# Two hybrid trunk layers on one core: the output projection in one pass over its weights, adaLN moved into the mixers

## The chip, the cores and the metric

The kernel runs on one NeuronCore of a Trainium2 chip. The metric is device time in microseconds. In the text PE is TensorE, DVE is VectorE, ACT is ScalarE, POOL is GpSimd, and SP is the engine whose queue issues every DMA of this kernel.

## The reference, cut to what matters

Five tiles of 128 tokens (tile 0 the prompt, tiles 1 to 4 the samples), 1024 wide, go through two layers. `m` has six vectors of 1024 for each of the two conditions (prompt and sample).

```python
def trunk_layer(x, cond, lp, ctx):
    m = silu(cond) @ lp['w_ada'] + lp['b_ada']          # adaLN
    sh1, sc1, g1, sh2, sc2, g2 = jnp.split(m, 6, axis=-1)
    h = layer_norm(x) * (1.0 + sc1) + sh1
    o, new_ctx = mixing(h, lp, ctx)                     # S5 scan | neighbourhood attention | GQA, then @ w_out
    x = layer_norm(DEEPNORM_ALPHA * x + g1 * o, lp['ln1_g'], lp['ln1_b'])
    h = layer_norm(x) * (1.0 + sc2) + sh2
    a, gate = jnp.split(h @ lp['w_ffn_in'], 2, axis=-1)
    f = (silu(a) * gate) @ lp['w_ffn_out']
    x = layer_norm(DEEPNORM_ALPHA * x + g2 * f, lp['ln2_g'], lp['ln2_b'])
    return x, new_ctx
```

## The kernel before

Every product of fp32 operands is made of three matmuls of a high and a low part (`mm3`, L309), so each weight block that arrives is split (`split`, L280): a copy on ACT makes the high part, a subtraction on POOL or DVE the low part. `wload` (L293) loads 512 KB into one of three `wr` buffers and splits it into two blocks in the `wh` and `wl` rings of seven each.

One layer runs like this (`layer`, L1349). First come 18 GQA units (`pipelined`), and after each of them `between` (L1405) gives out some steps of the scan, of the remaining input projections and, at units 6 to 11 of layer 0, the six adaLN units in `todo`. Then comes neighbourhood attention (NA) in ten units with the rest of the scan between them. Then `wout` (L1463), then `ffn` (L1716). A unit of adaLN (`ada`, L358) is one vector and one half: eight slices of w_ada of 256 KB, 32 small matmuls, a PSUM copy on ACT, a transpose, an addition on DVE. After the second half of vector 2 or 5 (the gates) a copy on DVE, another transpose, a second copy and a DMA store the gate rows.

`wout` works in two groups, tiles 2, 1, 0 and then 3, 4. For each group and each half of 512 columns it loads and splits all of w_out's blocks for that half, four loads of 512 KB, and multiplies. The results are gated and added to the residual on DVE (L1497, L1498). Then follow for each tile of the group `post_ln` (L1277), a second normalisation, and `ffn_in_tile` (L1535), which transposes, modulates, and builds the operands of the FFN. Between the second group's matmuls and its LayerNorms stand three adaLN units (L1500; one word: `ADAW`), vector 5 of this layer and the start of the next layer's. In layer 1 only two are left.

`ffn` runs 22 blocks of `ffn_in` (the first two by `ffn_in_plain`, whose first halves need only tiles 2, 1 and half of 0) in six parts; after each part its share of w_ffn_out is applied to all tiles: a multiplication by the gate row and an addition per tile and half, both on DVE (L1755 to L1762). From the third block on one step of `ffn_side` is given out per block: one adaLN unit (up to vector 4 of the next layer) and one step of the scan's tables.

The order of instructions on each engine is that of the program, changed by the framework's planner, which runs a timeline of its own with priorities (attention units have a higher one). Each engine and SP's queue then keep their order.

Of the kernel before, what the change touches and what calls it, by code (L numbers as in the profile page):

```python
# [16 lines left out]
D = 1024  # L17
# [140 lines left out]
class Build:  # L158
# [7 lines left out]
    ADAN = (0,) * 6 + (1,) * 6 + (0,) * 6  # L166
# [126 lines left out]
    def wload(self, src, lo_eng=None):  # L293
# [8 lines left out]
        return [self.wsplit(raw[:, c:c + 512], lo_eng) for c in range(0, n, 512)]  # L302

    def wsplit(self, src, lo_eng=None):
        hi, lo = [self.wp.tile([128, 512], F32R, name=self.nm(t), tag=t, bufs=self.NW) for t in ("wh", "wl")]
        self.split(src, hi, lo, lo_eng)
        return hi, lo
# [50 lines left out]
    def ada(self, l, M, vec, half, wide=None, side=False):  # L358
# [35 lines left out]
        if vec in (2, 5) and half == 1:  # L394
            gc = self.smallp.tile([128, 2, KD], F32, name=self.nm("gc"), tag="gc", bufs=1)
            nc.vector.tensor_copy(gc, modc[:, vec].rearrange("p k c -> p c k"))
            pt = bank[0:16, 256:384]
            nc.tensor.transpose(pt, gc.rearrange("p c k -> p (c k)"), self.ident)
            row = (self.ev(n=128) if side else self.zt(128))[0:16]
            nc.vector.tensor_copy(row, pt)  # L400
            nc.sync.dma_start(gates[vec // 3].rearrange("c (k p) -> (c k) p", p=128), row)
# [947 lines left out]
    def layer(self, l, A, xsrc, T, nxt, tab, todo):  # L1349
# [55 lines left out]
        def between(n):  # L1405
# [12 lines left out]

        self.pipelined(units, 1, between)
        for _ in fill:  # L1420
            pass
        Ns = [self.na_prep(l, 0, zqk[0], znv)]
# [23 lines left out]
        for _ in ssm:  # L1446
            pass
        return self.wout(l, M, mx, xsrc, nxt)
# [14 lines left out]
    def wout(self, l, M, mx, xsrc, nxt):  # L1463
# [6 lines left out]
        ada = self.ada_side(l, M, nxt)  # L1470
        self.function(AF.Silu, self.after)
# [6 lines left out]
        junk = None  # L1478
        for group in self.GROUPS:
            for i in group:  # L1480
                xs[i] = self.k4()
                nc.sync.dma_start(xs[i], xsrc[i])
                sums[i] = self.columns("wsum")
            for n in range(2):
                cs = slice(n * 512, (n + 1) * 512)
                s2 = self.psS()
                ps = [s2[:, 0], s2[:, 1]] + ([self.psM()] if len(group) == 3 else [])
                for j, pair in enumerate((2, 3, 0, 1)):
                    w = self.wload(I["w_out"][l, pair // 2, n, pair % 2], self.LO[j % 2] and G)
                    for p, i in zip(ps, group):  # L1490
                        a = slice(i * 128, (i + 1) * 128)
                        for kk in range(2):
                            k = 2 * pair + kk
                            self.mm3(p, mh[:, k, a], ml[:, k, a], *w[kk], j + kk == 0, j + kk == 4)
                for p, i in zip(ps, group):
                    cd = 0 if i == 0 else 1
                    V.tensor_tensor(out=p, in0=p, in1=row(("g", cd), M["gates"][0, cd])[:, cs], op=ALU.mult)  # L1497
                    self.residual(xs[i][:, cs], p, sums[i][n], ALPHA)  # L1498
            self.ada_wide = False
            for _ in range(self.ADAW[min(self.GROUPS.index(group), 1)]):  # L1500
                next(ada, None)
            self.ada_wide = True
            for i in group:
                get = self.xs if i < 3 else self.ys
                xn = get(n=512), get(n=512)
                junk = junk or (self.k4(),)
# [397 lines left out]
```

## Time and profile before

| | us |
|---|---|
| median of 3 runs | 1804.81 (1793.88 to 1805.54) |
| profiled execution | 1804.75 |
| its span, first to last instruction | 1802.7 |
| PE busy | 1655.2 (92%) |
| DVE busy | 1224.2 (68%) |
| ACT busy | 822.3 (46%) |
| POOL busy | 762.5 (42%) |
| mean granted clock | 0.95 |

The page shows the busy share of each engine in 40 slices of 45 us, and the granted PE clock as a share of full speed (0.5 is 1.2 GHz, 1.0 is 2.4 GHz). The windows give the same sums for any stretch, the waits who stood still for whom, and the orders of time single instructions.

### The profile page before, as it was taken

How to read it: one execution, taken by the hardware profiler on the slowest of the kernel's cores; microseconds unless marked ns; L12 is line 12 of the kernel's file. 1: busy time of each engine (PE TensorE's matmuls, PEld its weight loads, DVE VectorE, ACT ScalarE, POOL GpSimd, SP SyncE). 2: the span in 40 equal slices, each digit the busy share in tenths (PEclk: the TensorE clock that was granted, in tenths of full speed). 3: DMA queues.
4: the chain of work that ended last, by engine and by line, in shares of the span. 5: the costliest groups of instructions: out<-in, count | busy, mean ns of one | idle time of the engine just before them, and what ended most of it. 6: DMA issues, size and time to landing. Idle time of an engine off the chain costs nothing.

```text
span 1802.7 us, 31473 instructions
## 1 busy us (share of the span) xinstructions
PE 1655.2 (92%) x11624; PEld 1447.3 (80%) x11624; DVE 1224.2 (68%) x2460; ACT 822.3 (46%) x1796; POOL 762.5 (42%) x651
## 2 busy tenths in 40 slices
PE   5889899898899999999898989998979999999997
PEld 3778677676688888898797978976759898998995
DVE  5576536646778777678877555565476787876777
ACT  5435445556542334243246446665564342432433
POOL 3753303048434334346266232210684464363453
PEclk8889899889899999999999989998989999999999
DMA  8434767545453545332324243463542232222312
GB/s 311 121 110 116 231 202 203 149 158 178 149 161 115 176 126 184 109 115 72 122 77 165 91 115 86 121 183 113 178 161 83 91 98 64 89 74 68 105 60 82
DMA packets 183114, 234.90 MB, mean 130 GB/s; under 512 B 78960, under 2 KB 112048, under 8 KB 182960
## 3 DMA queue, kind: packets, MB, share of 16 engines
q1 hardware_dynamic: 182960, 232.88, 42.3%
q8 instruction: 92, 1.51, 0.3%
q14 instruction: 62, 0.51, 0.1%
HBM read 203.57 MB, written 29.39 MB: 129 GB/s over the span
## 4 chain that ended last, share of the span: by engine, by line
PE 66%; DVE 12%; DMA 10%; ACT 4%; issue 3%; POOL 2%; SPq 1%; POOLq 0%; DVEq 0%; ACTq 0%
PE psM L311 9%; PE psM L312 9%; PE psM L313 9%; PE psT L311 6%; PE psT L312 6%; PE psT L313 5%; DMA ev<-in_w_ada_dram 3%; PE psT L859 3%; PE psS L311 2%; PE psS L312 2%; PE psS L313 2%; PE psS L1157 2%; DMA wr<-in_w_ffn_in_dram 2%; PE psT L1184 2%; POOL wl L284 2%
## 5 line engine op out<-in xcount | busy, mean ns | idle before, releaser
L284 POOL TENSOR_TENSOR wl<-wr,wh 128x512 fp32r<-128x512 f32 x362 | 502.1, 1406 | 523.8 <-ACT wh L283 341.6
L283 ACT CAST wh<-wr 128x512 fp32r<-128x512 f32 x450 | 275.0, 620 | 388.4 <-PE psM L313 91.3
L311 PE MATMUL psM<-hh,wh 128*128 128x320 f32 x560 | 178.1, 318 | 2.5 <-DVE ev L400 1.2
L312 PE MATMUL psM<-hl,wh 128*128 128x320 f32 x560 | 176.2, 315 | 0.3 <-POOL hl L284 0.3
L313 PE MATMUL psM<-hh,wl 128*128 128x320 f32 x560 | 176.2, 315 | 0.0
L311 PEld LDWEIGHTS psM<-hh,wh 128*128 128x128 f32 x560 | 107.1, 191 | 5.5 <-DVE ev L400 1.8
L311 PE MATMUL psT<-hh,wh 128*128 128x320 f32 x352 | 110.0, 312 | 0.0
L312 PE MATMUL psT<-hl,wh 128*128 128x320 f32 x352 | 109.1, 310 | 0.0
L313 PE MATMUL psT<-hh,wl 128*128 128x320 f32 x352 | 109.0, 310 | 0.0
L313 PEld LDWEIGHTS psM<-hh,wl 128*128 128x128 f32 x560 | 107.0, 191 | 1.7 <-issue 1.6
L312 PEld LDWEIGHTS psM<-hl,wh 128*128 128x128 f32 x560 | 107.2, 191 | 1.1 <-POOL hl L284 0.6
L230 POOL TENSOR_TENSOR sm<-sm,mhalf 128x1 f32<-128x1 f32 (+2 forms) x46 | 55.9, 1217 | 96.3 <-DVE sm L260 51.7
L1638 DVE TENSOR_TENSOR ys<-ys,psM 128x320 f32<-128x320 f32 x140 | 65.0, 482 | 34.7 <-PE psM L313 32.9
L1638 DVE TENSOR_TENSOR ys<-ys,psT 128x320 f32<-128x320 f32 x140 | 65.1, 481 | 30.4 <-PE psT L313 29.0
L1160 DVE TENSOR_REDUCE psS<-psS 128x1 f32<-128x640 f32 x64 | 52.8, 828 | 45.3 <-PE psS L1157 43.7
L311 PE MATMUL psT<-b,wh 128*128 128x320 f32 x240 | 76.6, 319 | 7.3 <-DVE ys L1638 7.2
L311 PE MATMUL psM<-b,wh 128*128 128x320 f32 x240 | 76.4, 318 | 5.7 <-DVE ys L1638 5.6
L284 POOL TENSOR_TENSOR wl<-ws,wh 128x512 fp32r<-128x512 f32 x40 | 53.6, 1341 | 62.7 <-ACT wh L283 62.6
L311 PE MATMUL psM<-wh,hh 128*128 128x256 f32 (+1 forms) x232 | 73.8, 318 | 6.1 <-DVE sm L1329 2.9
L311 PE MATMUL psM<-wh,xs 128*128 128x512 f32 x190 | 75.1, 395 | 3.5 <-DVE k L1762 2.8
L311 PE MATMUL psT<-wh,xs 128*128 128x512 f32 x190 | 75.3, 396 | 2.9 <-DVE k L1762 2.9
L859 PE MATMUL psT<-ident,ys 128*128 128x128 f32 x440 | 75.4, 291 | 2.7 <-ACT ys L290 1.0
(439 smaller groups left out, 4904.8 us busy)
## 6 DMA issues: line engine op xcount, KB each, us to landing
wr<-in_w_ffn_in_dram SPq DMA_DIRECT2D x88, 512.0 KB, 3.8
ev<-in_w_ada_dram SPq DMA_DIRECT2D x112, 256.0 KB, 4.0
wr<-in_w_ffn_out_dram SPq DMA_DIRECT2D x40, 512.0 KB, 3.9
wr<-in_w_out_dram SPq DMA_DIRECT2D x32, 512.0 KB, 3.6
wr<-in_w_in_dram SPq DMA_DIRECT2D x28, 512.0 KB, 4.4
wa<-in_w_ada_dram SPq DMA_DIRECT2D x24, 512.0 KB, 4.6
k<-in_x_dram SPq DMA_DIRECT2D x10, 512.0 KB, 5.6
xs<-zqk SPq DMA_DIRECT2D x32, 160.0 KB, 5.1
```

The lines of the kernel that those rows point to most:

```text
L230: self.nc.gpsimd.tensor_tensor(out=o, in0=v, in1=self.mhalf.broadcast_to([128, v.shape[1]]), op=ALU.pow)
L283: nc.scalar.copy(hi, src)
L284: (lo_eng or nc.vector).tensor_tensor(out=lo, in0=src, in1=hi.bitcast(F32), op=ALU.subtract)
L311: nc.tensor.matmul(ps, lhsT=ah, rhs=bh, start=first, stop=False)
L312: nc.tensor.matmul(ps, lhsT=ah, rhs=bl, start=False, stop=False)
L313: nc.tensor.matmul(ps, lhsT=al, rhs=bh, start=False, stop=last)
L859: self.nc.tensor.transpose(pt[:, j * 128:(j + 1) * 128], s, self.ident)
L1157: nc.tensor.matmul(sp[:, b, 0:320], lhsT=qT[:, h * 128:(h + 1) * 128], rhs=kx[kv][:, b * 320:(b + 1) * 320], start=st, stop=en)
L1160: V.tensor_reduce(out=m, in_=sp[:, :, 0:320], axis=AX.XY, op=ALU.max, negate=True)
L1184: nc.tensor.matmul(pt[hh * 64:hh * 64 + 64, 256:384], lhsT=K["v"][:, j, kv * 64:kv * 64 + 64], rhs=PTs[j // 2][:, c0:c0 + 128], start=(j = ...
L1638: V.tensor_tensor(out=o, in0=x, in1=y, op=ALU.add)
```

## The change

- `wout` first multiplies the first half of the columns for all five tiles in five PSUM banks (one pass over half of w_out), then splits the second half's eight blocks and keeps them: seven in the rings, one in an `ev` buffer. The second half is multiplied for one tile at a time, in the order 2, 1, 0, then 3 and 4 between the LayerNorms of 2, 1 and 0.
- No adaLN stands in `wout`. Vectors 2, 3 and 4 are made in each layer's own mixers: a generator gives out parts of two slices after the GQA units from unit 5 on, each loaded one step ahead into a `wr` buffer, and parts of four slices in the ring buffers during NA. Each part ends with its own copy, transpose and addition. FFN's side now has vector 5 of its layer and vectors 0 and 1 of the next.
- The FFN's output sum is kept ungated: part 0 copies it on ACT, parts 1 to 3 add, part 4 adds, multiplies by the gate row and adds ALPHA times the saved tile, part 5 is as before. The tile is saved to DRAM (`xd`) after its LayerNorm and reloaded by halves in part 4.

```diff
-    ADAN = (0,) * 6 + (1,) * 6 + (0,) * 6
+    ADA0 = 5
...
+    def ada_parts(self, l, M, todo):
...
+        for vec, half in todo:
...
+            while k0 < KD:
+                n = 4 if self.ada_free else 2
...
+                    raw = self.wp.tile([128, n, 512], F32, name=self.nm("wa"), tag="wr", bufs=self.NRAW)
+                    nc.sync.dma_start(raw, wv[:, k0:k0 + n, c0:c0 + 512])
...
+                yield
+                bank = self.psM()
...
+                mrow = self.zt(128)
+                nc.scalar.copy(mrow, ps)
+                nc.tensor.transpose(pt, mrow, self.ident)
...
+            if vec == 2 and half == 1:
+                self.gate_rows(M, vec, bank, self.zt)
...
-            for _ in range(self.ADAN[n]):
-                if todo:
-                    self.ada(l, M, *todo.pop(0))
+            if n >= self.ADA0:
+                next(ada, None)
...
-        for _ in ssm:
+            if n:
+                next(ada, None)
+        for _ in itertools.chain(ada, ssm):
...
-        for group in self.GROUPS:
...
+        s2 = self.psS(), self.psS()
+        ps = [s[:, b] for s in s2 for b in range(2)] + [self.psM()]
+        pairs = 2, 3, 0, 1
+        for j, pair in enumerate(pairs):
+            w = pair, self.wload(I["w_out"][l, pair // 2, 0, pair % 2], G)
+            for p, i in zip(ps, self.WORD):
+                product(p, i, w, j == 0, j == 3)
+        ws = [(pair, self.wload(I["w_out"][l, pair // 2, 1, pair % 2], G, self.ev if j == 3 else None))
+              for j, pair in enumerate(pairs)]
+        for p, i in zip(ps, self.WORD):
+            gated(0, i, p)
...
+        def second(i):
+            p = self.psM()
+            for j, w in enumerate(ws):
+                product(p, i, w, j == 0, j == 3)
+            gated(1, i, p)
+
+        def through(i):
...
+            nc.sync.dma_start(xd[i], xs[i])
+            self.ffn_in_tile(xn, i, M["modc"], H)
...
+        for i in self.WORD[:3]:
+            second(i)
+        for m, i in enumerate(self.WORD):
+            through(i)
+            for k in self.WORD[m + 3:m + 4]:
+                second(k)
...
+    WORD = (2, 1, 0, 3, 4)
...
+                x = xs[i][:, cs]
                 if part == 0:
...
+                    S.copy(x, ps)
+                elif part < len(PARTS) - 2:
+                    V.tensor_tensor(out=x, in0=ps, in1=x, op=ALU.add)
                 else:
...
+                        t = self.zt()
+                        nc.sync.dma_start(t, xd[i][:, cs])
+                        V.tensor_tensor(out=ps, in0=ps, in1=x, op=ALU.add)
+                        V.tensor_tensor(out=ps, in0=ps, in1=g[:, cs], op=ALU.mult)
+                        V.scalar_tensor_tensor(out=x, in0=t, scalar=ALPHA, in1=ps, op0=ALU.mult, op1=ALU.add)
...
-            for vec in range(5):
+            for vec in range(2):
...
-            todo = [(2 + n // 2, n % 2) for n in range(6)]
             for l in range(L):
+                todo = [(2 + n // 2, n % 2) for n in range(6)]
```

## Rows read from the trace of the kernel before

**Rows 1.** Page: busy tenths of PE in 40 slices, and the granted clock

```profile
PE   5889899898899999999898989998979999999997
PEclk8889899889899999999999989998989999999999
```

**Rows 2.** Windows: stretch, length, busy us (instructions) of each engine, clock, DMA share, GB/s

```profile
413.40:487.00 73.60, 59.20 (x428) 45.61 (x427) 59.78 (x120) 47.38 (x89) 51.68 (x41) 0.86 0.57 183
438.50:476.50 38.00, 23.60 (x234) 16.05 (x235) 32.03 (x68) 24.52 (x48) 24.45 (x21) 0.77 0.62 196
1322.60:1358.50 35.90, 23.70 (x206) 17.14 (x205) 27.16 (x63) 23.77 (x47) 25.27 (x22) 0.76 0.52 166
310.00:360.00 50.00, 41.65 (x286) 31.21 (x286) 34.87 (x100) 27.87 (x80) 3.42 (x9) 0.83 0.62 163
1060.00:1200.00 140.00, 137.33 (x1225) 122.92 (x1224) 80.61 (x213) 88.86 (x227) 32.02 (x42) 0.98 0.40 110
1200.00:1260.00 60.00, 53.23 (x332) 40.13 (x330) 37.95 (x101) 32.63 (x94) 5.67 (x10) 0.80 0.53 151
```

**Rows 3.** Order of time on PE: start us, us, line, operation, tiles, shape

```profile
437.88 0.39 PE L312 MATMUL psS<-wl,hh 128*128 128x512 f32 x1
438.11 0.39 PE L313 MATMUL psS<-wh,hl 128*128 128x512 f32 x1
...
456.00 0.90 PE L311 MATMUL psS<-hh,wh 128*128 128x320 f32 x2
...
502.35 0.31 PE L312 MATMUL psM<-hl,wh 128*128 128x320 f32 x1
502.49 0.31 PE L313 MATMUL psM<-hh,wl 128*128 128x320 f32 x1
...
1322.27 0.39 PE L313 MATMUL psS<-wh,hl 128*128 128x512 f32 x1
```

**Rows 4.** Waits of PE, 440:480 and 1326:1362: us in total, times, longest

```profile
PE psM L381 <- DMA ev<-in_w_ada_dram: 12.1, 7, 3.4
...
PE psM L381 <- DMA ev<-in_w_ada_dram: 8.2, 4, 3.5
```

**Rows 5.** Order of time on DVE: the plain FFN blocks' last multiplications

```profile
503.92 0.49 DVE L1712 TENSOR_TENSOR ys<-psT,ys 128x320 f32<-128x320 f32 x1
...
1382.28 0.48 DVE L1712 TENSOR_TENSOR ys<-psT,ys 128x320 f32<-128x320 f32 x1
```

**Rows 6.** Groups by shape, DVE, 410:490: count, busy us, mean ns, idle before

```profile
L1298 DVE SCALAR_TENSOR_TENSOR k<-k,sm,k 128x1024 f32<-128x1024 f32 x5 | 10.1, 2027 | 2.3 <-POOL sm L230 2.2
L1288 DVE SCALAR_TENSOR_TENSOR k<-k,sm,k 128x1024 f32<-128x1024 f32 x5 | 8.1, 1610 | 0.0
```

**Rows 7.** Instructions of L1298: duration min/median/max ns, first and last start us

```profile
L1298 DVE SCALAR_TENSOR_TENSOR k<-k,sm,k x19: 1274/1286/2315, 419.4 to 1794.8; 128x1024 f32<-128x1024 f32 x19
```

**Rows 8.** Chain that ended last, 440:480: start us, us, what

```profile
451.65 0.23 PE psM L386
...
461.65 0.57 PE psM L381 x16
```

**Rows 9.** Waits of PE, 140:320: us in total, times, longest

```profile
PE psM L381 <- DMA wa<-in_w_ada_dram: 5.0, 4, 3.2
PE psM L386 <- ACT zt L385: 5.0, 2, 3.1
PE psM L398 <- DVE gc L396: 2.0, 1, 2.0
```

**Rows 10.** Waits of PE, 480:960: us in total, times, longest

```profile
PE psS L381 <- DMA ev<-in_w_ada_dram: 4.2, 8, 1.5
PE psM L311 <- DVE k L1762: 2.8, 2, 2.5
```

**Rows 11.** Groups by line: count, busy us, mean ns, idle before and releasers

```profile
L284 POOL TENSOR_TENSOR wl<-wr,wh 128x512 fp32r<-128x512 f32 x362 | 502.1, 1406 | 523.8 <-ACT wh L283 341.6
...
L1755 DVE TENSOR_TENSOR psM<-psM,k 128x512 f32<-128x512 f32 x50 | 34.8, 695 | 26.6 <-PE psM L313 26.4
```

More of the change, by code (lines that the diff above doesn't have):

```diff
@@ L290, in evac, with wload @@
             self.nc.scalar.copy(out, in_)
-    def wload(self, src, lo_eng=None):
+    def wload(self, src, lo_eng=None, last=None):
         nc = self.nc
@@ L301, in wload, with wsplit @@
         nc.sync.dma_start(rv, src)
-        return [self.wsplit(raw[:, c:c + 512], lo_eng) for c in range(0, n, 512)]
-    def wsplit(self, src, lo_eng=None):
-        hi, lo = [self.wp.tile([128, 512], F32R, name=self.nm(t), tag=t, bufs=self.NW) for t in ("wh", "wl")]
+        return [self.wsplit(raw[:, c:c + 512], lo_eng, last if c + 512 >= n else None) for c in range(0, n, 512)]
+    def wsplit(self, src, lo_eng=None, place=None):
+        if place:
+            hi, lo = place(F32R), place(F32R)
+        else:
+            hi, lo = [self.wp.tile([128, 512], F32R, name=self.nm(t), tag=t, bufs=self.NW) for t in ("wh", "wl")]
         self.split(src, hi, lo, lo_eng)
@@ L394, in ada @@
         if vec in (2, 5) and half == 1:
[L395 to L401, printed above, removed]
+            self.gate_rows(M, vec, bank, self.ev if side else self.zt)
@@ new lines, in gate_rows @@
+    def gate_rows(self, M, vec, bank, place):
+        nc = self.nc
+        gc = self.smallp.tile([128, 2, KD], F32, name=self.nm("gc"), tag="gc", bufs=1)
+        nc.vector.tensor_copy(gc, M["modc"][:, vec].rearrange("p k c -> p c k"))
+        pt = bank[0:16, 256:384]
+        nc.tensor.transpose(pt, gc.rearrange("p c k -> p (c k)"), self.ident)
+        row = place(n=128)[0:16]
+        nc.vector.tensor_copy(row, pt)
+        nc.sync.dma_start(M["gates"][vec // 3].rearrange("c (k p) -> (c k) p", p=128), row)
@@ L1470, in wout @@
         ada = self.ada_side(l, M, nxt)
+        xd = self.dp.tile([NT, 128, D], F32, name=self.nm("xd"))
         self.function(AF.Silu, self.after)
@@ L1476, in row @@
             return rows[key]
-        junk = None
-        for group in self.GROUPS:
[L1480 to L1506, printed above, removed]
-                s = self.post_ln(xs[i], row("lg", I["ln1_g"][l]), row("lb", I["ln1_b"][l]), sums[i], junk,
-                                 self.LNW[i])
-                self.normalise(xs[i], xn, self.stats_of(xs[i], s, junk, "lsn"), self.NORMV[2])
-                self.ffn_in_tile(xn, i, M["modc"], H)
@@ L1511, in wout, with product @@
-        return self.ffn(l, xs, M, H, nxt, ada)
-    LO = (True, True)
-    GROUPS = ((2, 1, 0), (3, 4))
-    ADAW = (0, 3)
+        for i in self.WORD:
+            xs[i] = self.k4()
+            nc.sync.dma_start(xs[i], xsrc[i])
+            sums[i] = self.columns("wsum")
+        def product(p, i, w, first, last):
+            pair, blocks = w
+            a = slice(i * 128, (i + 1) * 128)
+            for kk in range(2):
+                k = 2 * pair + kk
+                self.mm3(p, mh[:, k, a], ml[:, k, a], *blocks[kk], first and kk == 0, last and kk == 1)
@@ new lines, in gated @@
+        def gated(n, i, p):
+            cs, cd = slice(n * 512, (n + 1) * 512), 0 if i == 0 else 1
+            V.tensor_tensor(out=p, in0=p, in1=row(("g", cd), M["gates"][0, cd])[:, cs], op=ALU.mult)
+            self.residual(xs[i][:, cs], p, sums[i][n], ALPHA)
+        s2 = self.psS(), self.psS()
[5 more added lines that the diff above has]
+                product(p, i, w, j == 0, j == 3)
@@ L1728, in ffn @@
         f0 = 0
-        for key, cd in (("gp", 0), ("gs", 1)):
-            row(key, M["gates"][1, cd])
         for part, nf in enumerate(PARTS):
```

54 lines of the change are left out of this document (45 added, 9 removed).

## The prediction

> **What bounds the kernel now.** I read the page first. TensorE (PE) stands at 8 or 9 tenths and more in nearly all of its slices [rows 1], so the time is its matmul stream plus the places where that stream stops or runs at the lower clock. In the page's slices PE and PEclk dip together around the end of each layer's output projection, in layer 0's attention, and at the ends of the run [rows 1]. So next the windows by stage [rows 2]: 1060 to 1200 us (layer 1's GQA units) is 98% PE, with nothing to hide new PE work behind; 310 to 360 and 1200 to 1260 us (the neighbourhood attention, NA, of the two layers) leave 8.4 and 6.8 us idle; the two stretches from the projection's last matmul to a full FFN stream, 438.5 to 476.5 and 1322.6 to 1358.5 us, leave 14.4 and 12.2 us idle and run at a mean clock of 0.77 and 0.76. The third view, PE's order of time, shows what stands in the first of these [rows 3]: the last projection matmul starts at 438.11, the first FFN product only at 456.00. The fourth, PE's waits there, names one releaser: the adaLN matmuls that the kernel queues at that place wait 12.1 and 8.2 us for their 256 KB weight loads [rows 4]. That view alone would promise 20 us. The fifth view, VectorE (DVE), says why it is not all to be had: from 413.4 to 487.0 us it is busy 59.8 of 73.6 us, 81% [rows 2], with the post-LayerNorm and FFN operands of five tiles. The FFN's first two blocks (the plain ones) are through at 503.92 and 1382.28 [rows 5]; these are the marks by which I measure a shorter tail.
>
> **The change part by part.** The sum is made against the profiled execution, 1804.75 us (span 1802.7 and 2.05 around it); the median of the runs shown is 1804.81, the same.
>
> *A. Projection and tail.* Matmuls stay 240 a layer. What goes: 8 of 16 loads of 512 KB and 16 of 32 weight splits a layer, each 1406 ns on GpSimd (POOL) [rows 11], 22.5 us a layer, and the adaLN units there (three in layer 0, two in layer 1). POOL and the loads are not what PE waits for while it projects, so for themselves they are worth nothing; they count through DVE, below. The new order ends its first-half pass 120 matmuls before the end. At 0.23 us each [rows 3] that is 438.3 - 27.6 = 410.7, and 1322.5 - 27.6 = 1294.9 in layer 1. Tile 2's second half is then complete 5.5 us later, the others every 5.5 us. Now DVE has all the LayerNorm work ahead of it: 59.8 us, plus 4.3 for six first-half operations of three tiles that were done earlier (3 x two of 0.7), less 6.3 that belongs after tile 4's first operand: 57.8. Of this, 5.5 us is stretching: the 1024-wide LayerNorm operations mean 2027 ns, or 1610 [rows 6], where the shortest takes 1274 [rows 7], five of each kind. So the work is 57.8 at the old share of 81%, 71.4 us, at worst, and 52.3 us at 100% at best. I take 52.3 at 92% (halfway between the tail's own 84% [rows 2] and full), 57 us, because POOL, whose splits ran beside the slow ones, loses 22.5 us just there. Then 2 us for the operand's split, and the plain blocks' second halves, 96 matmuls at 0.147 [rows 3], 14.1 us, and 1 us to the mark: 410.7 + 57 + 2 + 14.1 + 1 = 484.8 against 503.9, -19; in layer 1, 1369 against 1382.3, -13. A = **-32**, ends -42 (52.3) and -4 (71.4). The first halves fill part of the wait from about 447 on. The first FFN weights can be split only as the held second half comes free (8 splits, 11 us of POOL from about 434): done by 446, just hidden; uncovered, up to 6 us.
>
> The slow operations are those with two inputs in SBUF while POOL works. The Trainium skill ("SBUF — State Buffer", Who interferes with whom) says that a VectorE instruction with two SBUF inputs and a GpSimd instruction that reads SBUF exclude each other for a whole instruction. The trace agrees as far as 1274 against up to 2315 ns goes [rows 7]. By that rule the FFN's weight splits, now run beside the LayerNorms of tiles 0, 3 and 4, would keep three of the five tiles stretched, and A would be about 3 us a layer less, the sum -13 and the time 1792.
>
> *B. adaLN in the mixers.* A unit (one vector, one half) is 64 PE instructions, 16 take 0.57 us [rows 8], so 2.3 us. Cut into parts of two (GQA) or four (NA) slices, each part ends with a PSUM copy on ScalarE (ACT), a transpose of 0.23 [rows 8], and a hand-over PE to ACT to PE. Its price is not in the trace for this place: in layer 0's GQA it cost 5.0 us over six units [rows 9], in the dense FFN nothing over nine (the wait list there shows only their loads, 4.2 us [rows 10]). I take the mean over the fifteen, 0.33 us; the ends are 0 and 0.83. A part is then 0.56 above its matmuls.
> Layer 0 GQA: out go 6 x 2.3 and the waits 5.0 + 5.0 + 2.0 [rows 9], 25.8; in come three units, 6.9, twelve parts, 6.7, and the gate wait 2.0, together 15.6: -10. The loads are now issued one attention unit ahead, so their wait goes.
> Layer 0 NA: three units and six parts, 10.3, half of the 8.4 idle taken: +6. Layer 1 GQA: the same 15.6 with no cover: +16. Layer 1 NA: 10.3 less 3.4: +7. B = **+19**. Ends: +7 (no hand-over) and +37 (0.83).
> Queued behind a part's transpose on PE stand the next attention unit's scores; behind the gate row on SP's queue, the next loads.
>
> *C. FFN's side.* Layer 0 loses three of nine units (8 us and a third of 4.2), layer 1 gains two: -9 and +6, **-3** (0 to -5).
>
> *D. Output sum.* Of the 12 DVE operations per tile and half a layer, 8 remain and one copy goes to ACT: 40 x 0.695 [rows 11] = 28 us of DVE less a layer, in stretches where PE sets the pace. What PE waited there for that chain is 2.8 us [rows 10]: **-3**, ends 0 and -6. The last part but one now has three DVE operations, 2.1 us, against 12 matmuls of 0.23, 2.8: still hidden. Its reload of the saved tile (256 KB, two buffers, one needed every 2.8) I take as hidden behind them too; loads of that size kept PE waiting 3.5 us at the longest [rows 4], so bare it would be 0.7 us each, 14 in all.
>
> Sum: -32 + 19 - 3 - 3 = -19, so **1786 us**.
>
> **The rivals.**
> *Clean tail.* DVE runs without a break and without stretching, and hand-overs cost nothing: A -42, B +7, sum -41: 1764. For it: POOL's lighter load. Against: DVE never ran above 84% in either tail.
> *DVE keeps its share.* The chain through DVE, not PE's wait for the loads, sets the FFN's start; A is -4: 1786 + 28 = 1814. For it: the loads' waits lie under an 81% DVE. Against: fewer splits on POOL.
> *Hand-overs in the mixers*, the one on the slower side. In layer 0 two of six stood for 5.0 us [rows 9], 2.5 each. If each of the 36 new ones stands so, because the copy comes late in ACT's line, that is 36 x (2.5 - 0.33) = 78 more: 1864. It turns the change to slower by over 1% from 1.36 us each on. Against: nothing of it in the FFN.
> *SP's line.* The five tile stores wait for their LayerNorms ahead of the FFN's first weight loads; the first product then starts near 465 and A falls to -14: 1804. For it: SP issues in order. Against: three loads fit into buffers free since about 414.
>
> **How the numbers follow.** Forecast 0.45 (own range 1772 to 1800), clean tail 0.20, DVE's share 0.13, hand-overs 0.13, SP's line 0.09. A difference under about 1% (18 us) can't be told from none here. Faster by over 1% (below 1786.8): just over half of the forecast and the clean tail, 0.44. Slower: the hand-overs and a little of DVE's share, 0.15. The rest, 0.41, is within 1%. The range leaves out the hand-overs and the best of the clean tail: 1760 to 1815.
>
> **What would show it.** A: no adaLN matmul between the last projection matmul and the first FFN product, the latter within 8 us of the former, and the plain blocks through 19 and 13 us earlier against the projection's end. B: PE's waits for ACT at the part's transpose under 12 us in all, and a GQA stage longer by 16 us in layer 1. C and D: PE waits for DVE in the FFN near 0. A long wait for the copies, a late first FFN load, or a DVE at 81% would make the forecast wrong, each by its rival.

## The result

The changed kernel takes **1826.1 us** (median of 4 runs, 1823.3 to 1828.8) against 1805.2 for the kernel before beside it: a ratio of **1.0109, 95% interval 1.0071 to 1.0147**. It is about 20 us slower; the forecast was 1786, 19 us faster, with a range up to 1815. The profiled execution has a span of 1821.6 us.

The page of the changed kernel, busy tenths of PE and the granted clock in 40 slices (as [rows 1]):

```profile
PE   5889898896999999998888899988969999999997
PEclk9899998898899999999999999998989999999999
```

PE still stands at 8 and 9 tenths nearly everywhere. The dips at the projections' ends have not gone, they are deeper: the slices from 410 and from 1321 us stand at 6 tenths, where the deepest of [rows 1] between the run's ends is a 7. The order of time on PE shows the two tails (start us, us, line, operation, tiles, shape, idle before):

```profile
437.31 0.40 PE L317 MATMUL psM<-ev,hl 128*128 128x512 f32 x1
437.55 0.60 PE L471 MATMUL psT<-ident,xs 128*128 128x128 f32 x4
...
456.00 0.90 PE L315 MATMUL psS<-hh,wh 128*128 128x320 f32 x2 [1.63 <-ACT hh L284]
...
1341.14 0.39 PE L317 MATMUL psM<-ev,hl 128*128 128x512 f32 x1
...
1356.22 1.97 PE L471 MATMUL psT<-ident,xs 128*128 128x128 f32 x8 [13.40 <-ACT xs L274]
1359.52 0.90 PE L315 MATMUL psS<-hh,wh 128*128 128x320 f32 x2 [1.33 <-ACT hh L284]
```

No adaLN matmul stands between the last projection matmul and the first FFN product, as the prediction asked, and yet 18.7 and 18.4 us lie between them, where [rows 3] had 17.9. The wait has another name. PE's waits, 400 to 500 us, then 1034 to 1345 (us in total, times, longest):

```profile
PE psT L471 <- ACT xs L274: 13.4, 1, 13.4
...
PE psM L435 <- ACT zt L434: 2.8, 3, 1.7
```

13.4 us for the normalised tile 0 (and 13.4 once more in layer 1) have taken the place of the 12.1 and 8.2 us for adaLN weights in [rows 4]. The second line is the hand-over of the new adaLN parts: 2.8 us in all of layer 1's mixers.

The plain FFN blocks' marks, which answer to [rows 5]:

```profile
497.63 0.48 DVE L1789 TENSOR_TENSOR ys<-psT,ys 128x320 f32<-128x320 f32 x1
...
1401.24 0.48 DVE L1789 TENSOR_TENSOR ys<-psT,ys 128x320 f32<-128x320 f32 x1
```

They stand at 497.6 and 1401.2, where before had 503.9 and 1382.3. To place the loss, I cut every profile at four events of a layer: the first GQA scores, the first projection product, the mark, and the next layer's first scores or the end. All are starts in the order of time. In us:

| stage | before | after |
|---|---|---|
| layer 0, scores to projection (mixers) | 241.3 | 237.9 |
| layer 0, projection to mark (projection, tail) | 136.9 | 135.4 |
| mark to layer 1's scores (FFN) | 548.5 | 537.1 |
| layer 1, scores to projection | 199.1 | 233.7 |
| layer 1, projection to mark | 130.8 | 132.9 |
| mark to the end | 420.4 | 420.4 |

So the forecast of the tail (-19 and -13) came out at -1.5 and +2.1, and layer 1's mixers took 34.6 us more where 23 were forecast. The other stages are within 5 us of the sum's terms.

One caution on such a table: it is one execution of each kernel. The kernel with the ungated sum alone was profiled twice (u8 and u18 below), and its own mixers in layer 1 took 200.0 and 195.2. The same kernel can differ by 5 us in one stage, so such a difference proves nothing by itself; the times, with their intervals, decide.

### The profile page after: what moved, and what is told of

It is laid out like the page before. It is cut to its first block, busy times and chain, and to the rows that moved or that the text cites. A ratio compares the mean times of both kernels' runs of the same rounds, so it can differ in the third digit from the quotient of the medians.

```text
span 1821.6 us, 31446 instructions
## 1 busy us (share of the span) xinstructions
PE 1646.0 (90%) x11650; PEld 1442.8 (79%) x11650; DVE 1167.0 (64%) x2406; ACT 818.7 (45%) x1812; POOL 715.4 (39%) x619
## 5 line engine op out<-in xcount | busy, mean ns | idle before, releaser
L285 POOL TENSOR_TENSOR wl<-wr,wh 128x512 fp32r<-128x512 f32 x328 | 457.2, 1414 | 535.7 <-ACT wh L284 355.7
L284 ACT CAST wh<-wr 128x512 fp32r<-128x512 f32 x416 | 254.0, 620 | 361.5 <-DVE wr L1665 92.3
L315 PE MATMUL psM<-wh,hh 128*128 128x256 f32 (+1 forms) x286 | 95.5, 334 | 8.1 <-DVE ys L1308 3.3
L316 PE MATMUL psM<-wl,hh 128*128 128x256 f32 (+1 forms) x286 | 93.4, 326 | 2.8 <-POOL wl L285 2.8
L317 PE MATMUL psM<-wh,hl 128*128 128x256 f32 (+1 forms) x286 | 93.5, 327 | 0.0
L1665 DVE TENSOR_TENSOR ws<-wr,wr 128x512 f32<-128x512 f32 x40 | 34.9, 872 | 90.8 <-DMA wr<-in_w_ffn_in_dram 76.3
```

The source lines that it names most:

```text
L284: nc.scalar.copy(hi, src)
L285: (lo_eng or nc.vector).tensor_tensor(out=lo, in0=src, in1=hi.bitcast(F32), op=ALU.subtract)
L315: nc.tensor.matmul(ps, lhsT=ah, rhs=bh, start=first, stop=False)
L316: nc.tensor.matmul(ps, lhsT=ah, rhs=bl, start=False, stop=False)
L317: nc.tensor.matmul(ps, lhsT=al, rhs=bh, start=False, stop=last)
L1665: V.tensor_tensor(out=o, in0=x, in1=y, op=op)
```

## The experiments

Each kernel is told as an edit of the changed kernel or of the kernel before. Line numbers in rows are those of the kernel named.

**u1, the projection of before put back.**

```diff
-        for j, pair in enumerate(pairs):                     # one pass, five tiles
...
+        for group in ((2, 1, 0), (3, 4)):                    # as before, but no adaLN units
...
+            for n in range(2):
...
+                for j, pair in enumerate((2, 3, 0, 1)):
```

> The changed kernel with the projection of before (tiles in groups of three and two, w_out read and split twice), still without adaLN in it. If the one pass is worth what step A said (-32 us, some of it now hidden), the time rises from 1826 to about 1850. If its gain is lost behind the wait of 13.4 us that the trace of after shows in each tail, it is worth the 6 us of layer 0's mark alone: 1832. If the five residual loads that now stand ahead of the w_out loads on SP's queue are what made layer 1 late (+25 us between the last GQA matmul and the last projection matmul), the time falls to about 1805.

Measured: 1824.2 us, ratio to before 1.0131 (1.0107 to 1.0156), none of the three times expected; projection to mark 132.5 and 131.2 us against 135.4 and 132.9. In this kernel the one pass is worth nothing. The residual loads ahead of w_out are no cause of layer 1's lateness: with the loads back in their old places its mixers still take 237.7 us (233.7 in the changed kernel).

**u2, the output sum of before put back.**

```diff
-                if part == 0:
-                    S.copy(x, ps)
...
+                V.tensor_tensor(out=ps, in0=ps, in1=g[:, cs], op=ALU.mult)
...
+                if part == 0:
+                    V.scalar_tensor_tensor(out=x, in0=x, scalar=ALPHA, in1=ps, op0=ALU.mult, op1=ALU.add)
```

> The changed kernel with the output sum of before (gate on every part, no saved tile, no reload). Step D said -3 us for the change: 1829 here, and PE waits for DVE in the FFN's output parts come back (2.8 us in before). If the copies on ScalarE and the reload of the saved tile cost more than the 28 us of VectorE they take off, the time falls below 1823.

Measured: 1849.0 us. This is not a clean undoing: the gate rows of the FFN are now made by the first two adaLN units of the FFN's side, and a sum that is gated from the first part on must wait for them. The expectation had missed that. The FFNs take 546.8 and 438.1 us instead of 537.1 and 420.4; in layer 1 DVE waits 5.6 us for the gate row's load before its first gating, and PE 8.5 us for that sum. So the two edits need each other: with the units out of the tail, an ungated sum can go on without its gate and a gated one cannot.

**u3, layer 1's vectors back on layer 0's FFN side.**

```diff
-            for vec in range(2):
+            for vec in range(5):
...
-                todo = [(2 + n // 2, n % 2) for n in range(6)]
+                todo = [(2 + n // 2, n % 2) for n in range(6)] if l == 0 else []
```

> The changed kernel with layer 1's second-half vectors back on layer 0's FFN side, so that layer 1's mixers hold no adaLN at all; layer 0 stays as changed. Theory (the parts in layer 1's neighbourhood attention, their matmuls, loads and hand-overs, cost the 25 us that the trace shows between the last GQA matmul and the last projection matmul): that stretch falls from 155 to about 130 us, layer 0's FFN grows by 9 to 14 us, and the time is 1810 to 1815. By the steps B and C of the prediction the same edit is worth -23 + 9 = -14: 1812, with the GQA stage of layer 1 giving 16 of it. Rival (the residual loads or the projection's new order make layer 1 late): the stretch stays near 150 us and the time rises by the FFN's 9 us to 1835.

Measured: 1818.3 us, 1.0096 (1.0070 to 1.0123): 8 us less than the changed kernel by the medians and 2 by the ratios, each beside its own runs of the kernel before, and above the 1810 to 1815 expected. Layer 1's mixers fall from 233.7 to 204.2 us, and the FFN with its six more units grows from 537.1 to 562.0. So a unit costs 24.9 / 6 = 4.15 us in the dense FFN and some 5 in the mixers. The theory on where the 34.6 us lie holds for 29.5 of them; the profit of moving the units back is small, because they are paid for there too.

**u4 and u5, who holds tile 0's LayerNorm?** In the changed kernel POOL works like this ahead of the first FFN product (order of time, POOL, then DVE):

```profile
436.62 7.19 POOL L285 TENSOR_TENSOR wl<-wr,wh 128x512 fp32r<-128x512 f32 x5
443.78 2.48 POOL L285 TENSOR_TENSOR hl<-xs,hh 128x512 fp32r<-128x512 f32 x2
446.24 2.29 POOL L285 TENSOR_TENSOR wl<-wr,wh 128x512 fp32r<-128x512 f32 x1
448.49 1.26 POOL L285 TENSOR_TENSOR ev<-wr,ws 128x512 fp32r<-128x512 f32 x1
449.71 0.55 POOL L231 TENSOR_TENSOR sm<-sm,mhalf 128x1 f32<-128x1 f32 x1
...
443.89 0.15 DVE L261 TENSOR_SCALAR sm<-sm 128x1 f32<-128x1 f32 x1
446.13 1.27 DVE L1342 SCALAR_TENSOR_TENSOR k<-k,sm,k 128x1024 f32<-128x1024 f32 x1
```

DVE's input for tile 0's last one-column power is there at 444.0, but POOL comes to it at 449.7: the FFN weights' splits, which the prediction called "just hidden", stand ahead in its line. u4 puts these splits on DVE; u5 leaves them on POOL and orders them behind the power.

```diff
-                self.split(rv[:, a], hi, lo, G)
+                self.split(rv[:, a], hi, lo, V)                        # u4
+                with self.tc.issue_after(self.behind[f].ins):          # u5
+                    self.split(rv[:, a], hi, lo, G)
```

> The changed kernel with the low halves of the plain FFN blocks' weights made on VectorE, not on GpSimd (8 of them a layer). Theory (tile 0's LayerNorm waits for its one-column power, which stands behind those splits in GpSimd's line): the wait of TensorE for the normalised tile falls from 13.4 us to 7 or less in each layer, the plain blocks end 6 us earlier, and the time is about 1816. Rival (VectorE's LayerNorm work alone sets it): the wait stays above 10 us, VectorE has 8 splits of 0.4 to 0.7 us more a layer, and the time is 1826 to 1834.

> The changed kernel with one order written into GpSimd's line: the low halves of the first plain FFN block's weights come behind tile 0's last one-column power, those of the second block behind tile 0's operand. Moving these splits to VectorE took 1.4 us off each layer's stretch only, and filled VectorE (10.0 of 10 us at 440 to 450). Theory (GpSimd's line holds tile 0's power by 5.8 us, 443.9 to 449.7): TensorE's wait for the normalised tile falls from 13.4 to about 8 us, the plain blocks end 4 to 5 us earlier in each layer, and the time is about 1817. Rival (the LayerNorm chain from the late second halves, tile 2's sums at 420.6, sets it, or the splits are then late): the plain blocks' mark moves by less than 1.5 us in each layer and the time is 1823 to 1829.

Measured: 1824.4 us and 1824.8. In u4 the wait falls to 11.1 us only, with DVE busy for 10.0 of 10 us from 440 on. PE's waits in u5, 400 to 500 us, and POOL's power there:

```profile
PE psT L471 <- ACT ys L274: 8.0, 2, 6.0
PE psT L471 <- ACT xs L274: 5.4, 1, 5.4
...
443.10 0.55 POOL L231 TENSOR_TENSOR sm<-sm,mhalf 128x1 f32<-128x1 f32 x1 [0.24 <-DVE sm L261]
```

The power came 6.6 us earlier, and PE waits 8.0 + 5.4 us instead of 13.4: the splits moved behind it are now late themselves, and projection to mark is 137.5 us, no shorter, which is what the rival expected. POOL's line was where the wait became visible, not what paces the tail. That theory fell.

**u6 and u7, the parts in the neighbourhood attention.**

```diff
-                    for j, raw in enumerate(raws):                      # u6: the first part's loads alone
-                        nc.sync.dma_start(raw, wv[:, k0 + j, c0:c0 + 512])
...
+                    if l in self.kept:
+                        raws = self.kept[l]
...
+                if self.ada_free and (vec, half, k0) != (4, 1, 4):      # u7: loads, but no product
...
+                    k0 += n
+                    continue
```

> The changed kernel; in the neighbourhood attention of each layer only the first adaLN part loads its weights, and the later ones multiply those again (the loads are left out, so the second-half vectors are not the reference's). The stretch from layer 1's last GQA matmul to the plain blocks' mark took 190.5 us before, 215.5 after, 192.9 with no part in layer 1's mixers. Theory (the loads crowd the DMA queues at a share of 0.8 to 1.0 and delay the attention's and the scan's own loads): 200 us or less. Rival (the parts' own PE work and hand-overs, with the order they force on the scan): 208 us or more.

> The changed kernel; in the neighbourhood attention of each layer the adaLN parts only load their weights, and the matmuls, copies, transposes and adds of all but the last are left out (the second-half vectors they make are the bias alone). If the loads are what costs, the stretch from layer 1's last GQA matmul to the plain blocks' mark stays at 208 us or more; if the parts' PE work and hand-overs cost, it falls to 200 us or less, near the 192.9 us without any part.

Measured: the stretch from layer 1's last GQA matmul to the mark is 217.2 us in u6 and 207.9 in u7 (215.5 in the changed kernel). Without their loads the parts cost as much as ever, although the DMA share reached 1.02 there (1205 to 1215 us). Without their PE work 7.6 us go, between the two cases expected; step B had 10.3 for the parts of this place. Crowded queues are ruled out as the main cause; the rest is not in this place alone, as u11 shows.

**u8 and u18, the ungated sum alone, on the kernel before** (the same kernel twice).

```diff
+                nc.sync.dma_start(xd[i], xs[i])
...
-                V.tensor_tensor(out=t, in0=ps, in1=g[:, cs], op=ALU.mult)
...
+                    S.copy(x, ps)
+                elif part < len(PARTS) - 2:
+                    V.tensor_tensor(out=x, in0=ps, in1=x, op=ALU.add)
...
```

> The kernel before with the ungated output sum alone (gate once, in the last parts, the tile saved before the FFN and loaded again). Step D said -3 us (0 to -6): 1798 to 1804 against 1801 to 1805. If the copy on ScalarE and the reload cost more than the 28 us they take off VectorE: above 1810. If what the changed kernel won between layer 0's plain blocks and layer 1's attention (11.4 us) is the sum's, not the three adaLN units': about 1785.

> The kernel u8 once more (before, with the ungated output sum alone), on the chip and beside the runs of u17: 0.995 of the time before, as in u8 (0.9925 to 0.9982). If that was chance: 1.000.

Measured: 1795.1 us, 0.9953 (0.9925 to 0.9982), and 1793.5 us, 0.9918 (0.9896 to 0.9940). This part of the change is a gain of 8 to 15 us, and **u18 is the fastest kernel of the study, faster than before and after**. But the gain is not where step D put it. PE's waits for DVE in layer 0's FFN add up to 22.8 us in u18 and 22.2 in before, and that stage took 550.3 against 548.5.

**u9 and u16, the adaLN units back in the tail** (on u3, three in layer 0, two in layer 1).

```diff
         for i in self.WORD[:3]:
             second(i)
...
+        for _ in range(3 if l == 0 else 2):            # u9: ahead of the last two second halves
+            next(ada, None)
...
         for m, i in enumerate(self.WORD):
             through(i)
             for k in self.WORD[m + 3:m + 4]:
                 second(k)
+            if m == 1:                                 # u16: behind them
...
+                for _ in range(3 if l == 0 else 2):
+                    next(ada, None)
```

> The kernel u3 (the changed kernel, layer 1's second-half vectors on layer 0's FFN side; 1818 us) with three adaLN units of layer 0 and two of layer 1 taken out of the FFN and put into the tail, between the third and the fourth second half of the projection, as many as the kernel before has there. By the stages of u3 and of the changed kernel a unit costs (562.0 - 537.1) / 6 = 4.15 us in the dense FFN. Theory (the LayerNorm chain sets the tail and TensorE stands there anyway, so units there are free; what the change took out was no cost): the plain blocks' marks stay within 2 us against the last GQA matmul, the FFNs get 12 and 8 us shorter, and the time is about 1798. Rival (their loads hold TensorE as the wait list of before says, 12.1 and 8.2 us): the marks come 12 and 8 us later and the time stays at 1818.

> The kernel u9 with its three and two units behind the last second half of the projection instead of ahead of the last two. In u9 TensorE waited 19.4 us for their loads in layer 0's tail and the plain blocks' mark came 22.8 us later than in u3. Theory (in the 13.4 us in which TensorE waits for tile 0's LayerNorm the units are free, as they were behind the grouped projection of before, whatever the wait list says): the marks are within 4 us of u3's against the last GQA matmul, and the time is 1798 to 1804. Rival (24 loads of 256 KB come too late for that gap): layer 0's mark is 10 us or more later and the time is 1812 to 1820.

PE's waits, 400 to 500 us, of u9 and of u16:

```profile
PE psM L385 <- DMA ev<-in_w_ada_dram: 19.4, 11, 2.9
```

```profile
PE psM L385 <- DMA ev<-in_w_ada_dram: 11.4, 6, 4.8
...
PE psT L471 <- ACT xs L274: 0.5, 1, 0.5
```

Measured: 1829.3 us in u9 and 1806.4 in u16, against 1818.3 in u3. u9 is slower than either case expected: the units hold up the last two tiles, and projection to mark is 154.6 us, 20.3 more than in u3, against 14.7 won in the FFN. In u16 the same units wait 11.4 us for the same loads, nearly the 12.1 of [rows 4], and yet the stage is only 4.2 and 0.9 us longer than in u3, while the FFNs get 11.9 and 3.3 us shorter. (Counted from the last GQA matmul, as the expectation had it, the marks are 5.9 and 1.7 us later than u3's, where 4 was allowed.) PE's wait for tile 0 is down to 0.5 us. The adaLN wait lies in the time in which PE would have waited for the LayerNorm anyway. This is the heart of the case. The time is 2 us above the range expected, so the units were cheap there, not free.

**u10, a shorter LayerNorm.**

```diff
-        if eng == "vector":
+        if eng == "vector" and self.lnfull:                 # False for the LayerNorms behind the projection
             V.scalar_tensor_tensor(out=x, in0=x, scalar=m, in1=lg, op0=ALU.add, op1=ALU.mult)
...
```

> The changed kernel with one of the two 1024-wide VectorE operations of each LayerNorm after the projection left out (the mean and the gain are not applied, so the output is not the reference's): 5 x 1.27 to 2.07 us of VectorE a layer, three of them ahead of the first FFN product. Theory (the tail is paced by the LayerNorms' chain over VectorE, ScalarE and GpSimd): TensorE's wait for the normalised tile falls from 13.4 us by 3 to 6 us, and the plain blocks' mark comes 4 to 6 us earlier in each layer. Rival (TensorE, or the FFN's weights, set it): wait and mark move by less than 1.5 us.

PE's wait, 400 to 500 us:

```profile
PE psT L472 <- ACT xs L274: 8.5, 1, 8.5
```

Measured: the wait falls from 13.4 to 8.5 us in both layers, and projection to mark from 135.4 to 129.2 and from 132.9 to 130.8. The tail follows the LayerNorm's chain, fully in the wait and in layer 0's mark, in part in layer 1's.

**u11, three of layer 1's six units back.**

```diff
-            for vec in range(2):
-                for half in range(2):
+            for vec, half in ((0, 0), (0, 1), (1, 0), (1, 1), (3, 1), (4, 0), (4, 1)):
...
-                todo = [(2 + n // 2, n % 2) for n in range(6)]
+                todo = [(2 + n // 2, n % 2) for n in range(6 if l == 0 else 3)]
```

> The changed kernel with three of the six units of layer 1's mixers left there (those of the GQA stage), the other three, which the changed kernel does in the neighbourhood attention, back on layer 0's FFN side. From layer 1's first GQA scores to the plain blocks' mark the kernel before took 329.9 us, u3 (no unit there) 332.8, the changed kernel (six) 366.5. Step B said 16 us for the units in GQA and 7 for those after it: 349. If the units in the neighbourhood attention are what costs too much: 345 to 350. If those in GQA cost more than priced (26 of the 34 us, as is left after the 8 us that leaving out the others' matmuls gave): 355 to 360.

Measured: 353.0 us from first scores to mark, between the two cases, so 20.2 us for the three units in GQA (16 priced) and 13.5 for the three behind it (7 priced). Both were too cheap, the second by a factor of two.

**u12 and u14, layer 0's units in parts, on u8.**

```diff
-            for _ in range(self.ADAN[n]):
-                if todo:
-                    self.ada(l, M, *todo.pop(0))
+            if n >= 5:                                  # u12; in u14 twice
+                next(ada, None)
...
```

> The kernel u8 (before, with the ungated sum; 1795 us) with layer 0's six mixer units as the changed kernel has them, in parts, three in GQA and three in the neighbourhood attention; projection, tail and layer 1 as before. Step B gave -10 and +6 for this, -4: 1791. The changed kernel's stages show 19 us less in layer 0's GQA and 20 more from there to the first FFN product; if those 20 belong to the parts alone: 1796; if part of them is the projection's new order (tile 0's second half complete after 192 of 240 projection products, where the grouped order has tiles 2, 1 and 0 after 144): 1785 to 1790.

> The kernel u12 (before, with the ungated sum and layer 0's units in parts) with two parts in each attention unit instead of one, so that all six units of layer 0 are done in its GQA stage and none in its neighbourhood attention. By u12's stages (375.2 us in layer 0 against 379.9 in u8, three units in each place), and by the 6.7 us and 4.5 us that a unit cost in layer 1's GQA and neighbourhood attention: no gain, layer 0 at 373 to 380 us and 1793 to 1803 in all. If the neighbourhood attention is the bad place in layer 0: 362 to 368 us and about 1787.

Measured: 1800.8 us, 0.9967 (0.9945 to 0.9989), and 1802.1, 0.9991 (0.9962 to 1.0020), neither below u8. First to last scores took 21 us less in u12 than in u8 (149.6 to 170.9), and 16.5 of them came back between there and the mark. Where in layer 0's mixers the units stand is not what matters.

**u13, the grouped order without the second reading.**

```diff
-                    w = self.wload(I["w_out"][l, pair // 2, n, pair % 2], G)     # of u1
...
+                    if len(group) == 3:
+                        ws.append(self.wload(I["w_out"][l, pair // 2, n, pair % 2], G,
+                                             self.ev if (n, j) == (1, 3) else None))
+                    w = ws[j]                           # tiles 3 and 4: the held blocks for both halves
```

> The changed kernel with the grouped projection of u1, but tiles 3 and 4 multiply the held second-half blocks in both halves, so that no w_out block is loaded or split twice (the first-half blocks of tiles 3 and 4 are left out, so the output is not the reference's). Tiles 2, 1 and 0 are then complete after 144 projection products, as in u1 and before, and GpSimd has 16 splits a layer, as in the changed kernel. Theory (step A failed because the one pass completes the tile that the FFN waits for after 192 products instead of 144, which eats what the missing splits give): the plain blocks' mark comes 6 to 12 us earlier in each layer than after and u1, which both took 373 us in layer 0 from the first GQA scores to it. Rival (the LayerNorm chain takes as long whatever the order): 370 us or more.

PE's wait, 400 to 500 us:

```profile
PE psT L471 <- ACT xs L274: 6.3, 1, 6.3
```

Measured: 1816.3 us (one execution); the wait is 6.3 us in both layers instead of 13.4, and projection to mark 131.0 and 125.0 us, 4.3 and 7.8 less than in the changed kernel. Counted from the first scores, it is 1.8 us in layer 0 (371.5 us, which was the rival's case), and 6 in layer 1, the least that the theory expected. Against u1, which has the same order and splits every block twice, it is 1.5 and 6.2 us. The order does cost; it is not the whole of the 32 us.

**u15 and u17, the one pass with all vectors where before has them**; u17 has the tails' units as u16.

```diff
-            if n >= self.ADA0:
-                next(ada, None)
+            for _ in range(6 <= n < 12):
+                if todo:
+                    self.ada(l, M, *todo.pop(0))
...
-            for vec in range(2):
+            for vec in range(5):
...
```

> The changed kernel with all second-half vectors where the kernel before has them (layer 0's in its GQA stage, one product over all eight slices; layer 1's on layer 0's FFN side): what is left of the change is the one pass, the tail without adaLN, and the ungated sum. Against u8 (the sum alone, 1795) it adds the one pass and moves three and two units from the tails into the FFNs, 12 + 8 us by 4.15 each. Theory (the one pass and the emptied tail are worth about nothing, A = 0): 1812 to 1818. By step A as forecast (-32): about 1785 by A and C together.

> The kernel u15 (one pass, ungated sum, all second-half vectors where the kernel before has them) with three and two adaLN units in the tails again, behind the last second half. Against u18 on the same chip it differs by the one pass alone. u15 stands 0.8% above u8, 14 us, and five units cost 5 x 4.15 = 21 us in the FFN and about 5 in the tail by u16, so the one pass is worth about 2 to 6 us if that is all: 1790 to 1796, ratio to u18 0.996 to 1.000. If the one pass with its lighter GpSimd is worth what step A forecast: 0.983 or less. If it is worth nothing or costs: 1.000 or more.

Measured: u15 1810.2 us, 1.0031 (0.9995 to 1.0067), near the theory's 1812 and far from the 1785. u17 1801.1, 0.9978 (0.9960 to 0.9995), beside u18 with 0.9918: the one pass, with every unit in the same stage, **costs** 8 us by the medians and 11 by the ratios: the last of the three cases expected. Its projection to mark takes 137.0 and 130.2 us, where u18 takes 133.0 and 128.9. What makes up the rest the profiles don't tell: the profiled execution of u17 took 1811.6, 10 us over its median, and its largest excess, 11.1 us, lies in layer 1's mixers, where the two kernels do the same work and the clock differed (the rows at the end).

## Why the prediction failed

The runs make a ladder from the kernel before to the changed one. Ratios to before, times 1805; each step is good to some 6 us, the distance between u8 and u18, which are one kernel. The forecast of each step is put together from the prediction's own terms (a moved unit at the 3 us of step C, which has 9 for three and 6 for two):

| step | runs | measured us | forecast us |
|---|---|---|---|
| ungated sum (D) | u18 against before | -15 (u8: -8) | -3 |
| one pass (A) | u17 against u18 | +11 | together with the next: -32 + 15 |
| five units from the tails to the FFNs (A, C) | u15 against u17 | +10 | |
| layer 0's units in parts (B) | u3 against u15 | +12 | -4 |
| layer 1's six units into its mixers (B, C) | after against u3 | +2 (medians: +8) | +5 |
| sum | after against before | +20 | -19 |

**A is the step that failed**: -17 forecast for it and the units it frees, +21 measured, 38 us apart, where the whole forecast missed by 39; the other three misses (-12, +16 and -3) nearly cancel, which is luck. It failed in two places.

*The start.* The prediction let VectorE's 57 us of tail work begin at the pass's end, 410.7 us. The pass did end there. But a LayerNorm needs both halves of its tile, and until they are there VectorE has little to do. DVE's order of time in the changed kernel, and then its first LayerNorm instruction in before:

```profile
411.43 0.70 DVE L1552 TENSOR_TENSOR psM<-psM,k 128x512 f32<-128x512 f32 x1 [2.62 <-PE psM L317]
412.17 0.69 DVE L1357 SCALAR_TENSOR_TENSOR k<-k,psM 128x512 f32<-128x512 f32 x1
...
418.69 0.70 DVE L1552 TENSOR_TENSOR psM<-psM,k 128x512 f32<-128x512 f32 x1 [5.83 <-PE psM L317]
...
420.64 0.20 DVE L253 TENSOR_SCALAR sm<-sm 128x1 f32<-128x1 f32 x1
```

```profile
416.01 0.20 DVE L252 TENSOR_SCALAR sm<-sm 128x1 f32<-128x1 f32 x1
```

The first LayerNorm begins at 420.6 us, 10 us behind the 410.7 of the sum, and VectorE is busy for only 3.3 us between. Nor does it come near the sum's 92% behind that. Its last operation ahead of tile 4's first operand ends at 474.8. Here is the window up to there (us, DVE busy, clock, DMA share, GB/s), and then POOL's split of that operand:

```profile
410.70:474.80 64.10, 41.24 (x100) 0.80 0.30 103
```

```profile
476.49 1.73 POOL L285 TENSOR_TENSOR hl<-xs,hh 128x512 fp32r<-128x512 f32 x1
```

VectorE's share is 64%. It has less to do than the 52.3 us of the sum (four tiles' first halves are gated before the pass ends), and yet it takes 64.1 us where the sum had 57. The operand is ready at 478.2, where the sum had 469.7. From there to the mark it is 19.4 us, where the sum had 15.1: the first halves, begun at 456.0 and not at 447, still had 24 of their 96 products to run. The 8.5 and 4.3 us are the 12.8 by which the mark, 497.6, missed 484.8.

Counted from the first projection product, the first LayerNorm begins 58.4 us in (before 49.0), 56.1 in layer 1 (before 48.7). u17 and u18, with their units in the same stages, show it too: 55.8 and 52.0 against 47.3 and 46.5. The diff says so without any trace: the grouped order has tiles 2, 1 and 0 complete after 144 of 240 projection products; the one pass completes tile 2 after 144, tile 1 after 168 and tile 0, which the FFN waits for, after 192. PE interleaved tile 2's second half with tile 1's, so both were done at 419 to 420.

What the prediction said of the slow operations came true. DVE's groups, 410 to 490 us, as [rows 6]:

```profile
L1352 DVE SCALAR_TENSOR_TENSOR k<-k,sm,k 128x1024 f32<-128x1024 f32 x5 | 7.2, 1440 | 1.0 <-POOL sm L231 0.9
L1342 DVE SCALAR_TENSOR_TENSOR k<-k,sm,k 128x1024 f32<-128x1024 f32 x5 | 6.4, 1274 | 0.0
```

They are down from 2027 and 1610 ns to 1440 and 1274, 4.6 us a layer. From the first LayerNorm to the first FFN product takes 35.4 us, where before took 40.0. The gain is there, and the later start takes it back: 93.7 from the projection's first product to the FFN's first, against 88.9 before. (The rule of the Trainium skill, "SBUF — State Buffer", Who interferes with whom, would have kept three of five tiles stretched. Here one of the ten operations, at 438.17, took 2.07 us beside POOL's splits. At 446 us it was POOL's split that took 2.29 us while DVE's operation kept its 1.27: either of the two can be the one that takes longer.)

*The cover.* The prediction priced the adaLN waits of [rows 4] as partly real. u16 shows what they were: PE's time under the LayerNorm's chain, in which three and two units cost 4.2 and 0.9 us, where the FFNs had spent 11.9 and 3.3 on them. Taken out of it, they must be paid elsewhere. The fifth view, DVE at 81%, was read rightly as the reason for doubt; but a share is no chain. In the changed kernel DVE is busy 11.0 of the 18.7 us in which PE stands (437.3 to 456.0), POOL 15.9 and ACT 10.8: none is full, and yet nothing can start sooner, because tile 0's LayerNorm goes from one to the other. Among the rivals, *DVE keeps its share* named the place, with 0.13, and both its share of 81% and its A of -4 were still too good. *SP's line* did not come: the first FFN product's waits name the normalised tile, no load.

**B** was right in layer 0's sum in the profile (241.3 to 237.9, -3.4 for -4) but there by luck: first to last scores fell by 17.5 us where -10 was forecast, and the stretch behind them grew by 14.1 where +6 was. In time it was not right (+12 by u3 against u15, +2 to +9 by u12 against u8 and u18); the profiles spread that over several stages, and its cause stays open. In layer 1 it was 34.6 us for 23. The GQA stage alone got longer as forecast (first to last scores 119.3 to 134.0 us, +14.7 for +16), but a part of its input projections now runs behind it. The hand-over rival is out: 2.8 us of waits in all. (There are 38 new parts and not 36: each neighbourhood attention holds seven.) The windows of layer 1's mixers up to the last projection matmul, changed kernel and u3, show the rest (us, PE busy, clock, DMA share, GB/s):

```profile
1034.70:1341.10 306.40, 275.49 (x2279) 0.96 0.50 147
```

```profile
1060.10:1333.10 273.00, 252.79 (x1875) 0.94 0.41 121
```

PE is busy 22.7 us longer for six units, 3.8 each, where the prediction's matmuls and transposes come to 18 us (six times 2.3 and 18 of 0.23). Another 10.7 us are idle time, in no one wait. The prediction's cover, "half of the 8.4 idle taken" in layer 0 and 3.4 us in layer 1, was not to be had: here the idle time grew.

**C** was right in kind, -11.4 us in layer 0's FFN for -9, and mis-sized: 4.15 us a unit in layer 0 (6 units 537.1, 9 units 550.1 in u16, 12 units 562.0 in u3), where 3 was taken. In layer 1 it was less: u16's two units took 3.3 us off that FFN, 1.65 each.

**D** had the right sign, and the wrong size and place. Which wait its 8 to 15 us came from stays open: not the waits for DVE in the FFN, which are as long as before.

The range failed because its upper bound left out the rival on the slower side for a mechanism (the hand-overs) that was false, and let A end at -4. A bound of A from both sides would have had to ask what a LayerNorm that starts later costs; measured, that end was positive: +21 for A and the moved units together, +6 with their 15 us as forecast.

## What to carry to other kernels

A wait list names who came last, not what would go if that one came early: before taking work out of a gap, ask what else ends the gap, and treat work that sits there as hidden until an experiment shows otherwise. When an order of products changes, count after how many products the unit that the next stage waits for is complete. Price moved work by its whole cost in the new place (here mostly 4 to 7 us for 2.3 us of matmuls), and let a single-engine share never stand for a chain over three engines.

## What the hardware showed besides

One kernel, u8 and u18, was granted different clocks in the same stage in two executions, here layer 1 from the last GQA scores to the first projection product; the third row is u17, which does the same work there (window of us, PE busy, clock, DMA share, GB/s):

```profile
1170.80:1254.80 84.00, 78.42 (x536) 0.79 0.52 143
```

```profile
1170.80:1249.30 78.50, 70.59 (x535) 0.90 0.55 153
```

```profile
1174.00:1261.10 87.10, 78.41 (x538) 0.80 0.48 134
```

0.79, 0.90 and 0.80 are each a mean over stretches at 2.4 and at 1.2 GHz, with 7.8 us between the busy times of the first two for the same work. Together with such differences in other stages it is why single stages here are not read finer than 5 us. And a small instruction is as late as what stands ahead of it on its engine: tile 0's power takes 0.55 us on POOL and came 5.7 us after its input.
